# Attention probabilities: a diagonal of reciprocals in the transposing matmul, in place of a scaling pass

## The chip, the core and the metric

The kernel runs on one core of a Trainium2 chip. What counts is the device time of one execution in microseconds, as the median of three runs. The core has TensorE (PE, with its weight loads shown as PEld), VectorE (DVE), ScalarE (ACT), GpSimd (POOL) and SyncE (SP), which issues the transfers. Each engine works through its own queue in order.

## What is computed

Two layers of a diffusion backbone, over 1024 latent tokens and 256 context tokens. The first layer projects the input once and feeds two mixers side by side, a bidirectional chunked gated DeltaNet with 8 heads and windowed attention with 8 query heads on 2 key heads; the second layer is a gated linear recurrence. Both layers end in a squared-ReLU MLP. The part that matters here is the attention's softmax, which has one learned extra logit ("sink") per head:

```python
def _sink_softmax(scores, sink):
    s = jnp.broadcast_to(sink.astype(f32).reshape(1, KV_B, G_B, 1, 1), scores.shape[:-1] + (1,))
    p = jax.nn.softmax(jnp.concatenate([scores, s], axis=-1), axis=-1)
    return p[..., :-1]
...
        s_win = jnp.where(valid, jnp.einsum('bqkgd,bskd->bkgqs', q_blk, k_win) * scale, NEG_INF)
        s_ctx = jnp.einsum('bqkgd,bskd->bkgqs', q_blk, kc) * scale
        p = _sink_softmax(jnp.concatenate([s_win, s_ctx], axis=-1), sink)
        return (jnp.einsum('bkgqs,bskd->bqkgd', p[..., :span], v_win)
                + jnp.einsum('bkgqs,bskd->bqkgd', p[..., span:], vc))
```

A latent query block of 128 tokens sees up to three key blocks of its window and two blocks of cached context, so up to five key blocks of 128; a context query block sees two.

## The kernel before

**Stages.** The input projection and the triangular solves of the DeltaNet come first (to about 500 us), then one stage in which the DeltaNet's recurrence, the attention and the adaLN matmuls for later parts run interleaved (`dn_attention`, about 500 to 930 us), then the output projection, the MLPs and the second layer, which are long chains of three-term matmuls (L466 to L468, L546 to L548).

**The attention.** `attention` walks over 10 query blocks `a` and two halves `p` of the heads: 20 rounds. In a round, `att_scores` makes four score tiles of 128 queries (two key heads, two query heads each): matmuls L1918, L1921 and L1923 into a PSUM tile, a maximum on VectorE (L1925), an exp on ScalarE with the row sum (L1928) into an SBUF tile of tag `aP`, of which there are seven. Then the tiny tile `es` (128x4) takes the sink's share and the sums, and its reciprocal is taken (L1938). Line L1945 multiplies each of the four probability tiles by its column of `es`, two on VectorE and two on POOL (`ENG["P"]` is `"vvpp"`).

`att_out` follows one round later (`ATT_LAG` is 1). For each key block it transposes the four probability tiles on TensorE, with the identity as the moving operand (L1955), into one PSUM bank of tag `ps_w`, of which there are three, copies that bank to SBUF (tile `wraw`, on VectorE or ScalarE in turn), and multiplies it by the values for the two key heads (L1959). Over all rounds there are 84 key blocks: 5 for six of the query blocks, 4 for two and 2 for two, each twice. So there are 336 transposes and 168 matmuls on L1959. The last copy writes the result `x` to the mixer's output.

**The DeltaNet beside it.** Names in the rows: L1715, L1723 and L1731 prepare a chunk (`PT`, `Y`, `XW`), and L1762, L1769 and L1772 are a step of the recurrence, with copies of `VS` and the update of the state `S` on VectorE and ScalarE, and the products `St`, `QI`, `ek` and `kt` on POOL (a helper, L1638). `oA` and `oB` are outputs of the recurrence. The copies on ScalarE and VectorE are the helper lines L1643 and L1645. L1808 transposes a finished output. L300 are the adaLN matmuls, with weights `adaw` of 512 KB each from memory.

**What sets the order.** The parts are written as generators that are stepped in turn, each with a priority, and a list scheduler then fixes one order for each engine's queue. So an edit of the attention can also move instructions of its neighbours.

## Time and profile before

| | |
|---|---|
| Median of 3 runs | 3235.19 us (3234.73 to 3238.5) |
| The profiled execution | 3233.86 us, of which the span of the profile is 3232.1 us |
| Mean granted TensorE clock in it | 0.972 |
| PE busy | 3060.8 us, 95% |
| DVE, ACT, POOL busy | 1864.1 us, 1209.4 us, 1117.5 us |

How to read it: the busy share is an average over stages with different limits, so the stage that a change touches has to be looked at by itself. "Busy" for PE counts from an instruction's start to its modelled end, and neighbours overlap. The chain of work that ended last is followed back from the last instruction, at each step to what released it. A wait for several semaphores is put down to the engine that came last by the profile, which can be wrong by a little; where this matters the single instructions have to be read.

### The profile page before, as it was taken

To read this page: it belongs to the slowest core of one execution; us is meant where nothing else is said; L and a number is where in the kernel's file an instruction comes from. 1 tells how busy PE (TensorE), PEld (TensorE's weight loads), DVE (VectorE), ACT (ScalarE), POOL (GpSimd) and SP (SyncE) were. 2 spreads that over 40 slices of the span, in tenths; PEclk is the share of its full clock that TensorE was granted. 3 is DMA by queue.
4 is the path that set the end of the run, shared out by engine and by line. 5 is a ranking of instruction groups with operands and counts; after the bars stand their busy time and mean duration, and the time that the engine had idled before them with its cause. 6 is when DMAs were issued, how large, how long until landed. Compare 5 with 4: busy or idle time off the path is not lost.

```text
span 3232.1 us, 50272 instructions
## 1 busy us (share of the span) xinstructions
PE 3060.8 (95%) x19927; PEld 2485.3 (77%) x19927; DVE 1864.1 (58%) x2952; ACT 1209.4 (37%) x1972; POOL 1117.5 (35%) x781
## 2 busy tenths in 40 slices
PE   8989975889989999999999998999899999999999
PEld 5776764565557788888888877888678888888888
DVE  5548887576751522223777766888352222277776
ACT  5555433454331411112333335878241111133332
POOL 0000004454531432334767641000133333287664
PEclk9999986999999999999999998999999999999999
DMA  5346677536871233334534230110313333454332
GB/s 205 85 142 175 172 180 188 156 124 208 245 239 52 69 127 127 127 127 170 181 110 157 84 106 24 37 45 25 108 46 139 120 123 119 153 191 149 128 107 85
DMA packets 274058, 416.53 MB, mean 129 GB/s; under 512 B 77210, under 2 KB 139450, under 8 KB 269726
## 3 DMA queue, kind: packets, MB, share of 16 engines
q1 hardware_dynamic: 273822, 413.31, 40.0%
q8 instruction: 157, 2.57, 0.3%
q14 instruction: 79, 0.65, 0.1%
HBM read 290.80 MB, written 122.41 MB: 128 GB/s over the span
## 4 chain that ended last, share of the span: by engine, by line
PE 74%; DVE 8%; DMA 3%; issue 3%; ACT 2%; POOL 2%; SPq 1%; DVEq 0%; POOLq 0%; ACTq 0%
PE ps_mm L467 14%; PE ps_mm L466 14%; PE ps_mm L468 13%; PE ps_w L546 4%; PE ps_w L547 4%; PE ps_w L548 4%; PE ps_mm L547 4%; PE ps_mm L548 4%; PE ps_mm L546 4%; DVE prod L1600 2%; PE ps_ad L300 2%; PE ps_w L1959 1%; DVE Vinv L1601 1%; PE ps_w L1955 1%; PE ps_s L1918 1%
## 5 line engine op out<-in xcount | busy, mean ns | idle before, releaser
L466 PE MATMUL ps_mm<-hhi,whi 128*128 128x512 f32 (+2 forms) x2768 | 991.0, 359 | 24.7 <-ACT hhi L686 13.5
L467 PE MATMUL ps_mm<-hlo,whi 128*128 128x512 f32 (+2 forms) x2768 | 990.2, 358 | 8.8 <-POOL hlo L427 8.8
L468 PE MATMUL ps_mm<-hhi,wlo 128*128 128x512 f32 (+2 forms) x2768 | 987.6, 357 | 1.6 <-POOL wlo L457 1.6
L466 PEld LDWEIGHTS ps_mm<-hhi,whi 128*128 128x128 f32 (+1 forms) x2768 | 525.8, 190 | 111.1 <-ACT hhi L686 13.9
L467 PEld LDWEIGHTS ps_mm<-hlo,whi 128*128 128x128 f32 (+1 forms) x2768 | 526.2, 190 | 90.7 <-POOL hlo L427 11.6
L468 PEld LDWEIGHTS ps_mm<-hhi,wlo 128*128 128x128 f32 (+1 forms) x2768 | 526.3, 190 | 81.8 <-issue 6.0
L507 DVE TENSOR_TENSOR hid<-ffr 128x512 f32<-128x512 f32 (+1 forms) x192 | 148.9, 777 | 589.3 <-ACT ffr L506 507.1
L536 POOL TENSOR_TENSOR wlo<-ar,whi 128x1024 fp32r<-128x1024 f32 x96 | 246.7, 2584 | 268.7 <-ACT whi L535 251.2
L506 ACT ACTIVATE ffr<-ps_mm 128x512 f32<-128x512 f32 (+1 forms) x192 | 100.6, 525 | 548.2 <-PE ps_mm L468 546.5
L526 DVE SCALAR_TENSOR_TENSOR x<-ps_mm,mod,x 128x512 f32<-128x512 f32 x272 | 200.4, 746 | 82.8 <-PE ps_mm L548 82.6
L526 DVE SCALAR_TENSOR_TENSOR x<-ps_w,mod,x 128x512 f32<-128x512 f32 (+1 forms) x304 | 185.6, 632 | 100.7 <-PE ps_w L548 100.5
L511 POOL TENSOR_TENSOR tt<-hid 128x512 f32<-128x512 f32 x64 | 83.3, 1301 | 414.0 <-DVE hid L507 414.0
L453 ACT CAST whi<-wraw 128x512 fp32r<-128x512 f32 (+1 forms) x237 | 136.7, 617 | 197.9 <-PE ps_mm L467 84.1
L535 ACT CAST whi<-ar 128x1024 fp32r<-128x1024 f32 x96 | 98.0, 1051 | 292.6 <-PE ps_w L547 208.3
L457 POOL TENSOR_TENSOR wlo<-wraw,whi 128x512 fp32r<-128x512 f32 (+1 forms) x93 | 139.1, 1515 | 186.1 <-DVE hlo L687 93.0
L828 POOL MEMSET pad<- 128x2 f32 (+2 forms) x60 | 3.9, 119 | 439.8 <-DVE xc L846 200.0
L457 DVE TENSOR_TENSOR wlo<-wraw,whi 128x512 fp32r<-128x512 f32 x144 | 136.2, 972 | 33.2 <-ACT whi L453 33.0
L546 PE MATMUL ps_w<-pp,whi 128*128 128x256 f32 x512 | 143.6, 283 | 4.6 <-DVE x L526 4.6
L547 PE MATMUL ps_w<-pp,whi 128*128 128x256 f32 x512 | 143.4, 283 | 0.0
L548 PE MATMUL ps_w<-pp,wlo 128*128 128x256 f32 x512 | 141.0, 283 | 0.0
L511 POOL TENSOR_TENSOR tt<-hid,tt 128x512 f32<-128x512 f32 x64 | 85.3, 1333 | 118.2 <-DVE hid L507 118.0
L702 DVE SCALAR_TENSOR_TENSOR x<-ps_mm,mod,x 128x512 f32<-128x512 f32 (+1 forms) x40 | 25.9, 655 | 150.3 <-PE ps_mm L468 138.5
(416 smaller groups left out, 5890.1 us busy)
## 6 DMA issues: line engine op xcount, KB each, us to landing
adaw<-ada SPq DMA_DIRECT2D x80, 512.0 KB
dh<-hid SPq DMA_DIRECT2D x64, 640.0 KB
wraw<-ff SPq DMA_DIRECT2D x128, 256.0 KB
dt<-tt SPq DMA_DIRECT2D x32, 1024.0 KB
br<-dh SPq DMA_DIRECT2D x128, 256.0 KB
ar<-ff SPq DMA_DIRECT2D x128, 256.0 KB
br<-dt SPq DMA_DIRECT2D x128, 256.0 KB
wraw<-w_in SPq DMA_DIRECT2D x76, 256.0 KB
```

The costliest lines, as they stand in the source:

```text
L453: nc.scalar.copy(hv[:, o:o + half], raw[:, :half])
L457: e.tensor_tensor(lv[:, o:o + half], raw[:, :half], hv[:, o:o + half], op=ALU.subtract)
L466: nc.tensor.matmul(ps, whi[:, k, :], hhi[:, k, :], start=first and k == k0, stop=False)
L467: nc.tensor.matmul(ps, whi[:, k, :], hlo[:, k, :], start=False, stop=False)
L468: nc.tensor.matmul(ps, wlo[:, k, :], hhi[:, k, :], start=False, stop=last and k == k1 - 1)
L507: nc.vector.tensor_tensor(hid[i][:, t0:t0 + tw], r[:, :tw], r[:, :tw], op=ALU.mult)
L511: nc.gpsimd.tensor_tensor(t[:, j], x, y, op=ALU.subtract)
L526: nc.vector.scalar_tensor_tensor(xt[ti][:, o, :], ps[:, :tw], Gt[:, o, cc:cc + 1], xt[ti][:, o, :], op0=ALU.mult, op1=ALU.add)
L536: nc.gpsimd.tensor_tensor(lo[:, c], s, hi[:, c], op=ALU.subtract)
L546: nc.tensor.matmul(ps, ah, bh, start=first, stop=False, skip_group_check=True)
L547: nc.tensor.matmul(ps, ah, bl, start=False, stop=False, skip_group_check=True)
L548: nc.tensor.matmul(ps, al, bh, start=False, stop=last, skip_group_check=True)
```

## The change

The scaling pass over the four probability tiles goes. Instead, one POOL multiply per round writes `dg`, four diagonal matrices of 128x128 side by side: the identity times each of the four columns of reciprocals. Its tile `adg` has one buffer. `att_out` then uses an ordinary matmul with `dg` as the moving operand where it had a transpose with the identity: the probabilities are the stationary operand as before, and the product is the transposed tile with its columns already divided.

```diff
@@ -1936,23 +1936,20 @@
     nc.vector.tensor_tensor(es, es, sub(den), op=ALU.add)
     nc.vector.reciprocal(es, es)
-    for i in range(4):
-        P, sc = Ps[i][:, :w], es[:, i // 2, i % 2:i % 2 + 1]
-        e = ENG["P"][i]
-        if e == "a":
-            nc.scalar.activation(P, P, AF.Copy, scale=sc)
-        else:
-            (nc.vector if e == "v" else nc.gpsimd).tensor_scalar(P, P, sc, None, op0=ALU.mult)
-    yield Ps, kts
-
-
-def att_out(g, a, p, Ps, kts, mix):
+    dg = tl("adg", [128, 4, 128], 1)
+    nc.gpsimd.tensor_tensor(dg, g.con["ident"].unsqueeze(1).to_broadcast([128, 4, 128]),
+                            bc(es.rearrange("p k g -> p (k g)"), 128), op=ALU.mult)
+    yield Ps, dg, kts
+
+
+def att_out(g, a, p, Ps, dg, kts, mix):
...
-            nc.tensor.transpose(pt[:, 128 * j:128 * j + 128], Ps[j][:, 128 * i:128 * i + 128], g.con["ident"])
+            nc.tensor.matmul(pt[:, 128 * j:128 * j + 128], Ps[j][:, 128 * i:128 * i + 128], dg[:, j, :], start=True, stop=True,
+                             skip_group_check=True)
```

Since lines go, later lines move: L1955 becomes L1951, L1959 becomes L1956, and the multiply that makes `dg` is L1940.

The scheduler makes a slightly different order of it. POOL's queue in the middle of the stage, two rounds, before:

```order
L1638 TENSOR_TENSOR ek<-kt,sch 128x512
L1945 TENSOR_SCALAR aP<-aP,aes 128x640 x2
L1638 TENSOR_TENSOR kt<-kt,sch 128x512
L1638 TENSOR_TENSOR QI<-ql,qe 64x4x2x64
L1638 TENSOR_TENSOR St<-S_4629,egl 128x256
L1638 TENSOR_TENSOR QI<-ql,qe 64x4x2x64
L1638 TENSOR_TENSOR ek<-kt,sch 128x512
L1638 TENSOR_TENSOR kt<-kt,sch 128x512
L1945 TENSOR_SCALAR aP<-aP,aes 128x640 x2
```

and after the change:

```order
L1638 TENSOR_TENSOR ek<-kt,sch 128x512
L1638 TENSOR_TENSOR kt<-kt,sch 128x512
L1940 TENSOR_TENSOR adg<-con,aes 128x512
L1638 TENSOR_TENSOR QI<-ql,qe 64x4x2x64 x2
L1638 TENSOR_TENSOR St<-S_4629,egl 128x256
L1638 TENSOR_TENSOR ek<-kt,sch 128x512
L1638 TENSOR_TENSOR kt<-kt,sch 128x512
L1940 TENSOR_TENSOR adg<-con,aes 128x512
```

The two scalings of a round become one multiply. In the first of the two rounds it stands one place later than the scalings stood, behind `kt`, and the two `QI` products are no longer parted by `St`.

TensorE's queue there, from the preparation of a chunk up to the next step of the recurrence, before:

```order
L1955 MATMUL ps_w<-con,aP 128x128 x4
L1731 MATMUL ps_w<-XW,ek 64x64 x16
L1723 MATMUL ps_w<-XW,Y 32x32 x9
L1959 MATMUL ps_w<-wraw,Vtok 64x256 x2
L1723 MATMUL ps_w<-XW,Y 32x32 x7
L1955 MATMUL ps_w<-con,aP 128x128 x4
L1731 MATMUL ps_w<-XW,ek 64x64 x16
L1959 MATMUL ps_w<-wraw,Vtok 64x256 x2
L1955 MATMUL ps_w<-con,aP 128x128 x8
L1959 MATMUL ps_w<-wraw,Vtok 64x256 x2
L1955 MATMUL ps_w<-con,aP 128x128 x4
L1959 MATMUL ps_w<-wraw,Vtok 64x256 x2
```

and after the change:

```order
L1731 MATMUL ps_w<-XW,ek 64x64 x16
L1723 MATMUL ps_w<-XW,Y 32x32 x16
L1951 MATMUL ps_w<-adg,aP 128x128 x4
L1731 MATMUL ps_w<-XW,ek 64x64 x16
L1956 MATMUL ps_w<-wraw,Vtok 64x256 x2
L1951 MATMUL ps_w<-adg,aP 128x128 x8
L1956 MATMUL ps_w<-wraw,Vtok 64x256 x2
L1951 MATMUL ps_w<-adg,aP 128x128 x4
L1956 MATMUL ps_w<-wraw,Vtok 64x256 x2
L1951 MATMUL ps_w<-adg,aP 128x128 x4
L1956 MATMUL ps_w<-wraw,Vtok 64x256 x2
```

The first block of transposes has moved behind the whole of L1723, and the blocks and the value matmuls L1959 (now L1956) still take turns. In the other half of the period, where the recurrence steps, the order is the same as before.

## Rows read from the trace of the kernel before

**Rows 1.** The page's part 1: busy time, share of the span, instructions of each engine.

```profile
PE 3060.8 (95%) x19927; PEld 2485.3 (77%) x19927; DVE 1864.1 (58%) x2952; ACT 1209.4 (37%) x1972; POOL 1117.5 (35%) x781
```

**Rows 2.** The page's part 4: the chain that ended last, by engine.

```profile
PE 74%; DVE 8%; DMA 3%; issue 3%; ACT 2%; POOL 2%; SPq 1%; DVEq 0%; POOLq 0%; ACTq 0%
```

**Rows 3.** Busy time by window: length, engines (instructions), granted clock, DMA share, GB/s.

```profile
500.00:580.00 80.00, 55.99 (x641) 36.18 (x641) 60.31 (x113) 28.98 (x62) 37.48 (x29) 0.76 0.75 203
580.00:780.00 200.00, 175.03 (x2572) 123.20 (x2572) 134.32 (x267) 95.99 (x223) 102.24 (x82) 0.97 0.45 142
780.00:930.00 150.00, 145.45 (x1881) 84.65 (x1877) 106.28 (x263) 55.67 (x142) 68.83 (x57) 0.98 0.85 254
```

**Rows 4.** The same windows for line L1945 alone: the sum over them.

```profile
sum 430.00, DVE 27.57 POOL 70.25; mean DVE 9.19 POOL 23.42
```

**Rows 5.** Line L1945: its POOL instructions, and who waited for it (us, times).

```profile
L1945 POOL TENSOR_SCALAR aP<-aP,aes x40: 919/1880/2933, 545.1 to 922.0; 128x640 f32<-128x640 f32 x24, 128x512 f32<-128x512 f32 x8, 128x256 f32<-128x256 f32 x8
...
  PE ps_w L1769: 1.3, 4
```

**Rows 6.** PE's waits from 580 to 780 us: us in total, times, longest.

```profile
PE ps_ad L300 <- DMA adaw<-ada: 7.1, 2, 5.0
PE ps_w L1955 <- ACT oA L1643: 5.0, 4, 1.3
PE ps_w L1959 <- DVE wraw L1645: 4.0, 4, 1.7
PE ps_w L1955 <- ACT XW L1643: 3.8, 4, 1.3
...
PE ps_w L1769 <- POOL aP L1945: 1.3, 4, 0.3
```

**Rows 7.** Timeline around 668 us, VectorE and PE: start, us, engine, line, instruction.

```profile
667.82 0.43 DVE L1645 COPY VS<-ps_w 64x256 f32<-64x256 f32 x1
...
668.34 0.35 PE L1769 MATMUL ps_w<-VS,kt 64*64 64x64 f32 x5 [0.32 <-POOL aP L1945]
```

**Rows 8.** The chain from 500 to 930 us, pieces on L1945: start, us, what.

```profile
664.05 4.04 POOL aP L1945 x2
...
804.12 1.02 DVE aP L1945 x2
...
889.56 2.22 DVE aP L1945 x2
```

**Rows 9.** POOL's groups from 500 to 930 us: busy us, mean ns, idle before.

```profile
L1638 POOL TENSOR_TENSOR kt<-kt,sch 128x512 f32<-128x512 f32 x20 | 21.4, 1074 | 0.5
...
L1945 POOL TENSOR_SCALAR aP<-aP,aes 128x512 f32<-128x512 f32 x8 | 14.4, 1812 | 12.1 <-DVE aes L1938 8.8 <-DVE mod L310 3.2
```

**Rows 10.** Timeline of one block of L1955 and L1959, first part and whole.

```profile
671.90 0.33 PE L1955 MATMUL ps_w<-con,aP 128*128 128x128 f32 x1
...
671.90 0.66 PE L1955 MATMUL ps_w<-con,aP 128*128 128x128 f32 x4
...
673.29 0.44 PE L1959 MATMUL ps_w<-wraw,Vtok 128*64 128x256 f32 x2
...
673.29 0.65 PE L1959 MATMUL ps_w<-wraw,Vtok 128*64 128x256 f32 x4
```

**Rows 11.** Lines L1955 and L1959, matmuls: count, ns min/median/max, first and last start.

```profile
L1955 PE MATMUL ps_w<-con,aP x336: 270/273/476, 549.4 to 927.3; 128*128 128x128 f32 x168
...
L1959 PE MATMUL ps_w<-wraw,Vtok x336: 379/382/689, 554.5 to 930.3; 128*64 128x256 f32 x168
```

**Rows 12.** Windows for line L1955 alone: length, PE and PEld busy (instructions), clock.

```profile
500.00:580.00 80.00, 5.60 (x32) 3.52 (x32) 0.76 0.75 203
580.00:780.00 200.00, 32.37 (x196) 21.36 (x196) 0.97 0.45 142
780.00:930.00 150.00, 18.02 (x108) 11.64 (x108) 0.98 0.85 254
```

**Rows 13.** Tile VS: VectorE's copies from the state, ns min/median/max.

```profile
L1645 DVE COPY VS<-S x39: 273/600/2774, 505.1 to 915.9; 64x256 f32<-64x256 f32 x39
```

More of the change, by code (lines that the diff above doesn't have):

```diff
@@ L1987 @@
 ENG = dict(ek="p", kt="p", qe0="p", qe1="p", Y0="v", Y1="v", X0="a", X1="a", W0="a", W1="a", S0="a", S1="v", st="p", V0="a", V1="v",
-           o="a", pT="avava", ao="a", sq="v", os="v", P="vvpp")
+           o="a", pT="avava", ao="a", sq="v", os="v")
 def kernel(**inputs):
```

## Prediction, made before the changed kernel was run

> **What bounds the kernel now.** I read the page's busy line first: TensorE is busy 95% of the span [rows 1], and the chain that ended last lies on PE for 74% and on POOL for 2% [rows 2]. Of this chain only one stage can change, the DeltaNet and attention stage between 500 and 930 us, since every instruction that the diff touches stands there. I cut the stage in three by its engines [rows 3]. From 500 to 580 us PE is busy 56.0 of 80 us at a mean clock of 0.76. From 580 to 780 us it is busy 175.0 of 200: 25.0 us idle. From 780 to 930 us it is busy 145.5 of 150: 4.5 us idle, because the adaLN matmuls fill it. No other engine comes near: VectorE has 134.3 of 200 and 106.3 of 150, POOL 102.2 and 68.8. So the question at each edit is whether it touches PE, or something that PE waits for.
>
> **The scaling that goes.** L1945 takes 70.25 us on POOL and 27.57 on VectorE [rows 4], two instructions on each for every one of 20 rounds. Did PE wait for them? The list of those who waited for L1945 has one line of PE's matmuls, the DeltaNet line L1769 with 1.3 us [rows 5]; the transposes L1955, which read the scaled probabilities, are not in it. PE's own waits between 580 and 780 us say the same: the transposes wait for ScalarE's copies (oA 5.0 us, XW 3.8 us) and no row has them wait for aP [rows 6]. The 1.3 us put down to POOL's aP have another cause, too: POOL's pair of scalings starts at 664.05 and takes 4.04 us [rows 8], so it ends at 668.09, while PE's start at 668.34 follows VectorE's copy of VS, which ends at 668.25 [rows 7]. So the four pieces of 4.04 us that the chain shows for POOL (one stands in [rows 8]) aren't waits that end with the scaling. By its direct path the removal gives 0. What it can give is room on VectorE: the copy of VS stands behind a scaling pair and two maxima in VectorE's queue, and the 1.3 us of PE are really waits for it. I take 2 us for the stage (bounds 0 and 19.4 us, the latter the chain's four POOL pieces and its two VectorE pieces of 1.02 and 2.22 us [rows 8]).
>
> **The diagonal that comes.** Twenty POOL multiplies of 128x512, one operand broadcast along its rows, the other repeated four times. No row has this form. The nearest is kt, 128x512 with one broadcast operand, 1.07 us; the farthest is the scaling of 128x512 itself, 1.81 us [rows 9]. I take 1.07: 20 x 1.07 = 21 us in place of 70.25, ready after one instruction instead of after two in a row (4.04 us). POOL has idle time in all three stretches, so its price on the path is 0. There is one buffer for it: the multiply waits until the transposes of the round before have read the last diagonal, and QI and St of the recurrence stand behind it in POOL's queue. But it also needs the reciprocals, and these need the fourth exp of its own round. A round takes four aP buffers and there are seven, so this exp waits for the round before to release its first one, and that happens in the last block of the same set of transposes. The extra wait is then a few matmuls; bounds 0 and 20 x 0.66 = 13 us if a whole block each time [rows 10]. I take 0.
>
> **The matmul in place of the transpose.** This is on PE and decides the case. A transpose of 128 columns costs 0.11 us once PE streams: one is in flight 0.33 us, four 0.66, so three more take 0.33 [rows 10]. Is a plain fp32 matmul of the same shape dearer? The counts say so: L1955 issues 84 key blocks x 4 = 336 transposes and leaves 336 records; L1959 issues 84 x 2 = 168 matmuls and also leaves 336 [rows 11]. A plain fp32 matmul is thus two passes, a transpose one. The length of a pass: the two first passes of L1959, which run side by side in the two halves of the array, take 0.44 us, and with both second passes 0.65, so a pass of 256 columns adds 0.21, or 0.105 for 128 columns [rows 10]: the transpose's own rate. So the new matmul is 0.22 us where the transpose was 0.11: 0.44 us more per key block. Bounds: below, 0 (if the second pass were hidden; nothing in L1959's rows hides it); above, 0.66, a whole block as it stands alone. I take 0.44, and 84 x 0.44 = 37 us in all.
>
> The Trainium skill speaks here too: "TensorE: Matmul & The Clock Gate", section Terms, says that the transpose mode is four times faster for FP32. By it a block would rise from 0.44 to 1.76 us instead of 0.88, and the term would be an estimated 84 x 1.32 = 111 us. The rows above give a factor of two; the rule has its place among the rivals.
>
> **What hides it.** Divided over the three stretches by the transposes seen there [rows 12]: 32 of them are 8 blocks, 3.5 us; 196 are 49 blocks, 21.6 us; 108 are 27 blocks, 11.9 us. The order of work on PE is nearly what it was, so the waits that I know keep their places, and a wait shrinks only by what is added between the event that starts it and the instruction that waits.
> - 580 to 780 us: the four waits for oA (5.0 us) and the bank behind it have two transposing blocks ahead of them, 0.88 us each: 3.5 us. The four waits for VectorE's wraw (4.0 us) have one or two: about 2.6. The waits of L1769 (1.3 us) have one: all of it. The 3.8 us for XW stand in front of the transposes, and the 7.1 us for adaLN loads have few of them: 0 [rows 6]. Hidden 7.4, and 2 from VectorE's room: 21.6 - 7.4 - 2 = 12.
> - 780 to 930 us: 4.5 us are idle at all. I take half as cover, 2.4: 9.5 remain.
> - 500 to 580 us: PE is idle 24 us; the clock is low, so a block can cost twice its 0.44 us. I take 2 of 3.5 as hidden: 1.5.
>
> Sum 12 + 9.5 + 1.5 = 23 us. The profiled execution took 3233.86 us, 1.76 more than its span and 1.3 less than the median of the three runs. Forecast 3233.9 + 23 = 3257. Its own range: if the first two stretches hide everything and the third its 4.5 us, 11.9 - 4.5 = 7.4, that is 3241; if nothing is hidden, 3271.
>
> **Rivals.**
> 1. Faster: VectorE and POOL set the pace and PE's 95% is padding. For it: VectorE's copies VS<-S are 0.27 us at best, 0.60 at the median and 2.77 at worst [rows 13], so other work stretches them, and POOL's load falls by 49 us. Then the 19.4 us of scaling on the chain go, four diagonals of 1.07 come back, 15 us are won, and PE's 37 us lie in waits up to 2 us in the last stretch: 3233.9 - 15 + 2 = 3221. It wins once more than 22 of the 37 us are hidden and the whole 15 are real. Against it: the transposes wait for aP nowhere, and 11.9 us meet only 4.5 idle ones.
> 2. No difference: the hidden part and VectorE's room just balance the 37 us, or the two-pass matmul costs no more than a transpose here: 3234. Against it: the counts of records.
> 3. Nothing hidden, 3271, the end of my forecast's own range and counted in it.
> 4. A matmul dearer than two passes: at four times the transpose's 0.11 us each of 84 blocks grows by 1.32 us, 111 us in all, less some 15 of cover: 3330. Against it: the records and the pass time of L1959. This is the result that the Trainium skill's rule above would give.
>
> **How the numbers follow.** Forecast (3241 to 3271) 0.78; rival 1 0.09; rival 2 0.11; rival 4 0.02. About 0.2% (6.5 us around 3235) is what a measurement of this kernel can tell from no change. So slower 0.79 (the forecast with rival 4, less its lowest edge), same 0.12, faster 0.09. The range runs from the upper edge of rival 2, 3236, to 3271: the forecast and a little of rival 2, about 0.8.
>
> **What would show it.** After the change L1951 should leave 672 matmul records, not 336, with four matmuls taking some 1.1 us; no L1945 on POOL or VectorE, and 20 multiplies near 1.07 us on POOL. PE's busy time should rise by about 35 us and the stage end 23 us later; from 780 us on PE should have next to no idle time. POOL's and VectorE's busy time should fall by some 49 and 28 us with nothing gained by it. I am wrong if L1951 leaves 336 records, if its blocks are as short as before, or if the stretch from 580 to 780 us gets shorter, since then VectorE or POOL set its pace.

## The result

The changed kernel takes 3255.97 us (median of 4 runs, 3253.44 to 3258.53), against 3236.14 us for the kernel before beside it. The ratio is 1.0061, with a 95% interval of 1.0043 to 1.0078. So it is slower by about 20 us. The forecast was 3257 us, with the range 3236 to 3271.

The span and the first part of the changed kernel's page, to stand beside [rows 1]:

```profile
span 3253.3 us, 50889 instructions
PE 3091.4 (95%) x20263; PEld 2529.6 (78%) x20263; DVE 1843.6 (57%) x2912; ACT 1208.9 (37%) x1972; POOL 1071.1 (33%) x761
```

TensorE is busy 30.6 us longer, VectorE 20.5 us less and POOL 46.4 us less. The 336 extra instructions on PE (20263 against 19927) are the second passes. The windows of [rows 3] now:

```profile
500.00:580.00 80.00, 55.86 (x705) 40.03 (x707) 58.52 (x110) 25.98 (x57) 33.92 (x26) 0.77 0.73 197
580.00:780.00 200.00, 188.69 (x2729) 145.09 (x2724) 118.50 (x245) 97.43 (x225) 69.35 (x69) 1.00 0.45 137
780.00:930.00 150.00, 143.84 (x1802) 90.50 (x1800) 93.42 (x224) 53.13 (x134) 54.21 (x49) 0.99 0.81 235
```

From 580 to 780 us PE's idle time fell from 25.0 to 11.3 us. Before 580 and from 780 us on it did not fall. The line of the new matmul, its matmuls and its weight loads: count, ns min/median/max, first and last start; and the POOL multiply that makes the diagonals:

```profile
L1951 PEld LDWEIGHTS ps_w<-adg,aP x672: 186/192/338, 550.2 to 954.7; 128*128 128x128 f32 x168
L1951 PE MATMUL ps_w<-adg,aP x672: 271/275/534, 550.4 to 954.8; 128*128 128x128 f32 x168
...
L1940 POOL TENSOR_TENSOR adg<-con,aes x20: 1039/1041/1822, 547.1 to 944.8; 128x512 f32<-128x512 f32 x20
```

336 matmuls leave 672 records where the transposes left 336 [rows 11]. The multiply takes 1.04 us at the median, and nobody is listed as waiting for it. A block of four matmuls, eight records, and two blocks in a row, from the timeline of PE (start, us):

```profile
677.58 1.16 PE L1951 MATMUL ps_w<-adg,aP 128*128 128x128 f32 x8
...
681.40 2.05 PE L1951 MATMUL ps_w<-adg,aP 128*128 128x128 f32 x16
```

A block takes 1.16 us where it took 0.66 [rows 10]; in a row a further one adds 0.89, which is 0.111 us for each pass. Over the whole stage, 500 to 960 us, the line and its predecessor, from the groups of the costliest instructions (busy us, mean ns | idle before). Before:

```profile
L1955 PE MATMUL ps_w<-con,aP 128*128 128x128 f32 x336 | 56.0, 290 | 11.4 <-ACT oA L1643 5.0 <-ACT XW L1643 3.8 <-DVE oB L1781 2.1
```

and after:

```profile
L1951 PE MATMUL ps_w<-adg,aP 128*128 128x128 f32 x672 | 95.7, 289 | 2.4 <-DVE oB L1781 1.3 <-ACT oA L1643 1.2
```

39.7 us of matmul came in, and 9.0 us of idle time in front of these instructions went. PE's waits from 580 to 780 us in the changed kernel, to compare with [rows 6], show the same:

```profile
PE ps_w L1731 <- ACT XW L1643: 3.4, 4, 1.8
PE ps_w L1956 <- DVE wraw L1645: 3.2, 4, 0.9
PE ps_ad L300 <- DMA adaw<-ada: 3.1, 1, 3.1
PE ps_w L1956 <- ACT wraw L1643: 0.7, 2, 0.5
PE ps_w L1951 <- ACT oA L1643: 0.3, 1, 0.3
```

The waits for `oA` fell from 5.0 to 0.3 us, those for adaLN weights from 7.1 to 3.1, and the wait of L1769 is gone. The waits for VectorE's `wraw` fell little, from 4.0 to 3.2, and those for `XW` moved from the transposes (3.8) to L1731 (3.4).

**Where the 20 us arise.** To compare the two traces at the same work, I cut them at the start of the 8th, 24th and 40th of the 40 steps of the recurrence (L1762). Windows of the kernel before between these steps, columns as in [rows 3]:

```profile
606.82:753.59 146.77, 129.94 (x2019) 96.86 (x2017) 104.03 (x206) 79.93 (x185) 79.02 (x64) 0.98 0.39 120
753.59:922.41 168.82, 162.18 (x2142) 94.83 (x2139) 118.48 (x289) 62.07 (x156) 80.51 (x66) 0.98 0.83 251
```

and of the changed kernel:

```profile
608.03:761.77 153.74, 145.95 (x2179) 116.82 (x2176) 95.17 (x192) 78.84 (x183) 55.14 (x56) 1.00 0.38 115
761.77:946.19 184.42, 177.73 (x2273) 110.55 (x2271) 110.89 (x267) 63.50 (x159) 63.44 (x57) 0.99 0.80 241
```

Up to the 8th step the changed kernel has lost 1.2 us. In the middle part PE does 16.0 us more, but its idle time falls from 16.8 to 7.8 us, so the part grows by 7.0 us only. In the last part PE does 15.6 us more, its idle time stays at 6.7 us, and the part grows by the whole 15.6. At the end of the stage 3 us come back, so the first matmul of the output projection starts 20.7 us later. After it nothing differs: the spans differ by 21.2 us.

**A third term, the clock.** The last columns but two of these windows are the granted clock, 1.0 for the upper level of 2.4 GHz and 0.5 for the lower of 1.2. It is a mean, so a stretch of length L at a mean clock c spent 2(1-c)L at the lower level. The two kernels from 580 us to the first matmul of the output projection, before:

```profile
580.00:943.50 363.50, 329.77 (x4492) 210.33 (x4492) 248.59 (x541) 156.62 (x372) 173.94 (x141) 0.97 0.63 192
```

and after:

```profile
580.00:964.20 384.20, 361.56 (x4832) 250.97 (x4827) 228.68 (x511) 158.47 (x376) 131.34 (x124) 0.99 0.61 184
```

The lower level fell from 22 to 8 us. One place shows how. In both kernels TensorE waits for a load of adaLN weights shortly after 580 us, then runs four matmuls of L300. Before (timeline; start, us, what, and the idle time ahead of it):

```profile
583.40 1.92 PE L300 MATMUL ps_ad<-adaw,sc 128*32 128x512 f32 x4 [4.96 <-DMA adaw<-ada]
```

and after:

```profile
586.06 1.05 PE L300 MATMUL ps_ad<-adaw,sc 128*32 128x512 f32 x4 [3.14 <-DMA adaw<-ada]
```

The same four matmuls took 1.92 us behind the longer wait and 1.05 behind the shorter one. The windows of these places show the granted clock (third number from the end): during the longer wait it fell, and the matmuls behind it ran at 0.50. Before, the wait and the matmuls:

```profile
578.40:583.40 5.00, 0.04 (x1) 0.00 (x0) 2.59 (x5) 1.71 (x4) 3.58 (x2) 0.86 0.81 242
583.40:585.30 1.90, 1.90 (x6) 0.23 (x6) 0.00 (x0) 0.00 (x0) 0.45 (x1) 0.50 0.97 379
```

and after, the matmuls:

```profile
586.06:587.00 0.94, 0.94 (x4) 0.14 (x4) 0.00 (x0) 0.00 (x0) 0.00 (x0) 1.00 0.79 322
```

The Trainium skill ("TensorE: Matmul & The Clock Gate", section "HAM oscillation — how this bites in real kernels") says that idle gaps of TensorE bring its clock down; these rows agree.

### The profile page after: what moved, and what is told of

The parts are those of the page before. It is cut to its first block, busy times and chain, and to the rows that moved or that the text cites. A ratio compares the mean times of both kernels' runs of the same rounds, so it can differ in the third digit from the quotient of the medians.

```text
span 3253.3 us, 50889 instructions
## 1 busy us (share of the span) xinstructions
PE 3091.4 (95%) x20263; PEld 2529.6 (78%) x20263; DVE 1843.6 (57%) x2912; ACT 1208.9 (37%) x1972; POOL 1071.1 (33%) x761
## 4 chain that ended last, share of the span: by engine, by line
PE 76%; DVE 8%; DMA 4%; issue 3%; ACT 2%; SPq 1%; POOL 1%; DVEq 0%; ACTq 0%; POOLq 0%
PE ps_mm L466 13%; PE ps_mm L467 13%; PE ps_mm L468 13%; PE ps_w L546 4%; PE ps_w L547 4%; PE ps_w L548 4%; PE ps_mm L547 4%; PE ps_mm L548 4%; PE ps_mm L546 3%; PE ps_w L1951 2%; DVE prod L1600 2%; PE ps_ad L300 2%; PE ps_w L1956 1%; DMA adaw<-ada 1%; DVE Vinv L1601 1%
## 5 line engine op out<-in xcount | busy, mean ns | idle before, releaser
L457 DVE TENSOR_TENSOR wlo<-wraw,whi 128x512 fp32r<-128x512 f32 x144 | 136.2, 973 | 33.9 <-ACT whi L453 33.7
L541 DVE TENSOR_TENSOR bl<-br,bh 128x1024 fp32r<-128x1024 f32 x56 | 101.6, 1814 | 12.0 <-ACT bh L540 10.7
```

The source lines that it names most:

```text
L457: e.tensor_tensor(lv[:, o:o + half], raw[:, :half], hv[:, o:o + half], op=ALU.subtract)
```

## The experiments

My theory after the result: TensorE's passes set the price, the exchange of the scaling for the diagonal is worth nothing, and idle time hides part of the passes. The first rival: the scaling's removal wins some 15 us, and the passes cost nearly all of their 40.

**All runs in one table.** Each ratio is to runs of the kernel before that were taken beside that kernel. It isn't the quotient of the medians, and can differ from it by a few us. The columns from "length" on are of one profiled execution each, which can lie up to 8 us from the median. They cover 580 us to the first matmul of the output projection and come from window rows like the two above. "Low" is the time at the lower clock level, good to 4 us, since the mean clock has two digits. "Work" is PE's busy time less half of "low": about what it would be at the upper level.

| Kernel | Median, us | Ratio to before (95%) | Length | PE busy | PE idle | Clock | Low | Work |
|---|---|---|---|---|---|---|---|---|
| before | 3236.14 | 1 | 363.5 | 329.8 | 33.7 | 0.97 | 22 | 319 |
| changed | 3255.97 | 1.0061 (1.0043 to 1.0078) | 384.2 | 361.6 | 22.6 | 0.99 | 8 | 358 |
| changed, again | 3252.21 | 1.0056 (1.0041 to 1.0072) | 385.9 | 362.3 | 23.6 | 1.00 | 0 | 362 |
| matmul alone | 3256.57 | 1.0065 (1.0051 to 1.0079) | 393.3 | 366.4 | 26.9 | 0.98 | 16 | 359 |
| half of the matmuls | 3242.32 | 1.0011 (0.9998 to 1.0024) | 372.9 | 349.1 | 23.8 | 0.97 | 22 | 338 |
| identity per round | 3237.37 | 1.0009 (0.9997 to 1.0021) | 371.1 | 337.0 | 34.1 | 0.94 | 45 | 315 |
| no division | 3223.14 | 0.9971 (0.9957 to 0.9985) | 353.4 | 326.0 | 27.4 | 0.97 | 21 | 315 |
| diagonal unread | 3231.73 | 0.9987 (0.9976 to 0.9997) | 360.0 | 327.8 | 32.2 | 0.97 | 22 | 317 |
| all scaling on VectorE | 3248.77 | 1.0048 (1.0029 to 1.0067) | 375.5 | 334.9 | 40.6 | 0.95 | 38 | 316 |
| division at the end | 3239.79 | 1.0011 (1.0002 to 1.0019) | 370.1 | 336.8 | 33.3 | 0.96 | 30 | 322 |
| transposed twice | 3251.32 | 1.0053 (1.0035 to 1.0071) | 382.7 | 354.0 | 28.7 | 0.99 | 8 | 350 |
| transposed thrice | 3283.55 | 1.0145 (1.0127 to 1.0162) | 414.4 | 390.9 | 23.5 | 0.98 | 17 | 383 |
| F32R, one pass | 3268.85 | 1.0099 (1.0083 to 1.0115) | 396.7 | 353.8 | 42.9 | 0.91 | 71 | 318 |
| F32R, twice | 3267.89 | 1.0108 (1.0088 to 1.0129) | 395.0 | 367.1 | 27.9 | 0.97 | 24 | 355 |

The work column sorts the kernels by passes: 315 to 322 us where the probabilities pass once, 338 with half of the second passes, 350 to 362 where they pass twice, 383 with three. What the time makes of it is decided by the idle and the low column.

### The matmul alone, scaling kept

```diff
-            nc.tensor.transpose(pt[:, 128 * j:128 * j + 128], Ps[j][:, 128 * i:128 * i + 128], g.con["ident"])
+            nc.tensor.matmul(pt[:, 128 * j:128 * j + 128], Ps[j][:, 128 * i:128 * i + 128], g.con["ident"], start=True, stop=True,
+                             skip_group_check=True)
```

> The kernel before, its scaling kept, with one edit: the transposes of the probabilities become plain fp32 matmuls by the identity. Theory (the second pass on TensorE sets the price, the scaling costs nothing): the whole rise of the changed kernel is here already, 3256 to 3261 us, with 672 matmul records and four matmuls of a block near 1.16 us. Rival (the scaling's removal is worth 15 us, and the second pass costs all of its 35 to 40 us): 3268 to 3275 us, since nothing pays for it here. If the rise were due to the diagonal or to the order of work, this would stay near 3236.

Measured: 3256.57 us, ratio 1.0065. The whole rise is here, with no diagonal in the program and the scaling still in it. The rival's 3268 to 3275 is excluded.

### No division at all

```diff
-    for i in range(4):
-        P, sc = Ps[i][:, :w], es[:, i // 2, i % 2:i % 2 + 1]
...
-            (nc.vector if e == "v" else nc.gpsimd).tensor_scalar(P, P, sc, None, op0=ALU.mult)
```

> The kernel before without the four scalings of the probabilities, transposes by the identity kept; this leaves the division by the sum out of the computation. Theory (nobody on the path waits for the scaling, some 2 us of room on VectorE at most): 3231 to 3236 us, VectorE's and POOL's busy time down by 28 and 70 us with TensorE's unchanged. Rival (VectorE and POOL set the pace of the stage): the 15 to 19 us of scaling on the chain go, 3217 to 3222 us.

Measured: 3223.14 us, ratio 0.9971 (0.9957 to 0.9985). That is 9 us faster by the ratio and 13 by the medians: more than the theory's 0 to 5, and only 1 us above the band of the rival, so this time by itself does not refute the rival. The identity per round, below, does. The gain is made between 500 and 580 us. The first transposes start at 533.7 us there (line L1948 of this kernel), while before they start at 549.4 [rows 11]:

```profile
L1948 PE MATMUL ps_w<-con,aP x336: 270/273/476, 533.7 to 922.7; 128*128 128x128 f32 x168
```

Once nothing divides, a transpose waits only for its own tile's exp, and the scheduler puts the first ones into time in which TensorE idles beside a busy VectorE. The fifth step of the recurrence then starts at 571.9 us against 586.2 before, and nothing further is won after it: of these 14 us, 10 are left where the output projection starts (933.4 and 943.5). So this kernel tests two edits at once, the scaling and the dependence of the transposes on the reciprocals. The change keeps that dependence, through the diagonal.

### The diagonal made and read by nobody

```diff
-            nc.tensor.matmul(pt[:, 128 * j:128 * j + 128], Ps[j][:, 128 * i:128 * i + 128], dg[:, j, :], start=True, stop=True,
-                             skip_group_check=True)
+            nc.tensor.transpose(pt[:, 128 * j:128 * j + 128], Ps[j][:, 128 * i:128 * i + 128], g.con["ident"])
```

(against the changed kernel)

> The changed kernel with its diagonal made on POOL and read by nobody, the probabilities transposed by the identity; this leaves the division by the sum out of the computation. It differs from the kernel before by the scaling that goes and the POOL multiply that comes. Theory (both are off the path): as without any division, 3231 to 3236 us. If the diagonal multiply delays the recurrence's work in POOL's queue: up to 13 us more than without any division, 3244 to 3249 us. Rival (VectorE and POOL set the pace): 3217 to 3225 us.

Measured: 3231.73 us, ratio 0.9987, within the theory's bounds. It has the same flaw: the transposes no longer wait for the reciprocals, and the fifth step starts at 572.9 us. Set against the kernel without division it prices the POOL multiply at about 5 us (0.9987 less 0.9971; 9 by the medians), with intervals that overlap.

### The second pass alone taken away

To keep the dependence, this kernel makes in each round an identity of its own, in the diagonal's tile, at the diagonal's cost, and transposes by it:

```diff
-    nc.vector.reciprocal(es, es)
+    nc.vector.tensor_scalar(es, es, 0.0, None, op0=ALU.mult)
...
-                            bc(es.rearrange("p k g -> p (k g)"), 128), op=ALU.mult)
+                            bc(es.rearrange("p k g -> p (k g)"), 128), op=ALU.add)
...
-            nc.tensor.matmul(pt[:, 128 * j:128 * j + 128], Ps[j][:, 128 * i:128 * i + 128], dg[:, j, :], start=True, stop=True,
-                             skip_group_check=True)
+            nc.tensor.transpose(pt[:, 128 * j:128 * j + 128], Ps[j][:, 128 * i:128 * i + 128], dg[:, j, :])
```

(against the changed kernel)

> The changed kernel with the second pass alone taken away: the reciprocal becomes a product with zero and the POOL multiply an addition to the identity, so that each round makes an identity of its own in the diagonal's tile at the diagonal's cost and time, and the transposes by it wait for it as the matmuls do; this leaves the division by the sum out of the computation. Theory (the price is the second pass, the exchange of scaling for diagonal is worth about nothing as long as the transposes still wait for the reciprocals): 3233 to 3238 us, and the changed kernel's 20 us more are all second passes. Rival (the scaling's removal is worth 9 us by itself, as the kernel without division suggests): 3225 to 3229 us, and the second passes cost some 29 us. If the wait for the one diagonal buffer costs: above 3240 us.

Measured: 3237.37 us, ratio 1.0009 (0.9997 to 1.0021): 3 us more than before, with zero in the interval. The rival's 3225 to 3229 is excluded. So with the dependence kept, the exchange of the scaling for the diagonal wins nothing, and the second pass is worth 1.0061 less 1.0009, some 17 us, out of 40 us of matmul. The moved order of TensorE is in this price too: as in the changed kernel, the first block of transposes stands behind the preparation of the chunk here, and idle time (34.1 us against 33.7 before) is not hidden by it.

This kernel and the one before it both leave out the scaling and make a tile of the diagonal's size at its cost. They differ in whether the transposes wait for it. So that dependence is worth 1.0009 less 0.9987, some 7 us (6 by the medians), with intervals that only touch: much of what the kernel without division won.

### The same work from plain transposes: twice and thrice

```diff
-            nc.tensor.transpose(pt[:, 128 * j:128 * j + 128], Ps[j][:, 128 * i:128 * i + 128], g.con["ident"])
+            for _ in range(2):
+                nc.tensor.transpose(pt[:, 128 * j:128 * j + 128], Ps[j][:, 128 * i:128 * i + 128], g.con["ident"])
```

(and with `range(3)`; scaling kept, run beside the changed kernel once more)

> The kernel before with every transpose of the probabilities issued twice into the same place, scaling kept: 672 single passes, TensorE's work as in the changed kernel, nothing else new. Theory (the price is TensorE's passes, whatever their form): 37 us more of TensorE's work, about half of it covered as in the changed kernel, 3252 to 3261 us. If the plain fp32 form, its weight load or the diagonal costs by itself: 3236 to 3246 us here.

> As the one with every transpose twice, but three times: 1008 passes, twice the added work, some 74 us. Theory (waits of TensorE and clock hide a fixed amount, 11 us of idle time and some 6 us of low clock, and the first 37 us have used it up): the second 37 us cost nearly in full, 30 to 37 us above the kernel with every transpose twice, 3284 to 3295 us. Rival (a fixed share of about half is hidden, since waits for other engines give way again): 3270 to 3278 us.

> The changed kernel once more beside the kernels with repeated transposes, for a closer interval and its granted clock. Theory: 3253 to 3259 us, a clock of 0.973 or more where the kernel before has 0.968 to 0.973, and no more than 3 us from the kernel with every transpose twice. Rival (scaling in exchange for diagonal is worth the 9 us that the kernel without division gained): 9 us below that kernel.

Measured: 3251.32, 3283.55 and 3252.21 us, each up to 1 us under its band, with the differences as the theory had them. Twice costs 17 us (ratio 1.0053), the change beside it 18 us (1.0056), and thrice 47 us (1.0145). The first addition of passes costs 17 us, the second, of the same size, 32 us by the medians and 30 by the ratios. The windows of these two kernels from 580 us on (twice first, then thrice) show why:

```profile
580.00:962.70 382.70, 354.02 (x4856) 242.78 (x4855) 249.15 (x546) 158.91 (x376) 175.01 (x143) 0.99 0.60 184
```

```profile
580.00:994.40 414.40, 390.94 (x5121) 275.77 (x5119) 237.30 (x545) 157.99 (x376) 177.27 (x144) 0.98 0.55 168
```

From the kernel before to twice, PE's idle time goes from 33.7 to 28.7 us and the low clock from 22 to 8. From twice to thrice only 5 us more of idle time go, the low clock wins nothing (8 to 17 us), and the length grows by 31.7 of 36.9 us more busy time. So over these two additions what hides passes is a nearly fixed amount, and not a share of half. That twice and the change agree within 1 us also says that the plain fp32 form, the diagonal and the scaling all together are worth next to nothing beside the count of passes. Singly they are not separated: the changed kernel has 8 us more work in the table than twice, and 6 us less idle time.

### Half of the matmuls

Tiles 0 and 1 through a diagonal of two blocks, tiles 2 and 3 scaled on VectorE and transposed:

```diff
-    for i in range(4):
+    dg = tl("adg", [128, 2, 128], 1)
+    nc.gpsimd.tensor_tensor(dg, g.con["ident"].unsqueeze(1).to_broadcast([128, 2, 128]), bc(es[:, 0, :], 128), op=ALU.mult)
+    for i in range(2, 4):
...
+            if j < 2:
+                nc.tensor.matmul(pt[:, 128 * j:128 * j + 128], Ps[j][:, 128 * i:128 * i + 128], dg[:, j, :], start=True, stop=True,
+                                 skip_group_check=True)
+            else:
+                nc.tensor.transpose(pt[:, 128 * j:128 * j + 128], Ps[j][:, 128 * i:128 * i + 128], g.con["ident"])
```

> Half of the change: tiles 0 and 1 of the probabilities are divided in a plain matmul by a diagonal, tiles 2 and 3 are scaled on VectorE and transposed. 336 second passes are halved to 168. Theory (a price for each second pass): about half of the rise, 3243 to 3250 us. If waits hide the first ones, as they would if idle time of TensorE covers a fixed amount, then less than half: 3236 to 3243 us. Rival (VectorE's or POOL's load decides): POOL has lost its scaling and VectorE keeps its own, so 3225 to 3236 us.

Measured: 3242.32 us, ratio 1.0011 (0.9998 to 1.0024): 4 us by the ratio and 6 by the medians, less than half of the rise either way, just under the theory's lower end and in the case it named for it, that waits hide the first passes. With the runs above: half of the added passes cost 4 to 6 us, all of them 17 to 20, double 47.

### All scaling on VectorE

```diff
-           o="a", pT="avava", ao="a", sq="v", os="v", P="vvpp")
+           o="a", pT="avava", ao="a", sq="v", os="v", P="vvvv")
```

> The kernel before with all four scalings of a round on VectorE and none on POOL: POOL loses its 70 us, VectorE's 28 us double. Theory (nobody on the path waits for the scaling): within 4 us of before, 3232 to 3240 us. If POOL's share of the scaling holds the stage up, the four scalings end sooner (4 x 0.69 us in place of 4.04 us) and it is faster, 3224 to 3231 us. If VectorE sets the pace, 28 us more on it cost 10 to 28 us: 3246 to 3264 us.

Measured: 3248.77 us, ratio 1.0048, 13 us slower by the medians and 15 by the ratio. The theory's "within 4 us" fell; it came out as in the case in which VectorE sets the pace. Its 80 scalings take 0.55 us at the median (first fence), and two of PE's waits from 580 to 780 us, not seen in [rows 6] at that size, are now for the exp that stands behind VectorE's maxima, and for VectorE's copy of `VS` (second fence):

```profile
L1945 DVE TENSOR_SCALAR aP<-aP,aes x80: 345/547/555, 547.1 to 933.1; 128x640 f32<-128x640 f32 x48, 128x512 f32<-128x512 f32 x16, 128x256 f32<-128x256 f32 x16
```

```profile
PE ps_s L1918 <- ACT aP L1928: 3.9, 4, 1.3
PE ps_w L1769 <- DVE VS L1645: 2.0, 5, 0.5
```

PE's work is what it was (316 us), but its idle time rose by 7 us and the low clock by 16. So VectorE is not free: more load on it costs. Where it costs is read from the waits and not tested by itself, since the order of TensorE's work moved too. Less load on VectorE, as in the change, won nothing that could be measured.

### F32R, one pass and two

F32R is a 4-byte type like fp32, in which this kernel holds the mask of the scores. Probabilities and diagonal in F32R make the plain matmul a single pass (`tl("aP", [128, 640], ..., F32R)`, and the same for `adg`):

```diff
-        P = tl("aP", [128, 640], g.NB["aP"])
+        P = tl("aP", [128, 640], g.NB["aP"], F32R)
...
-    dg = tl("adg", [128, 4, 128], 1)
+    dg = tl("adg", [128, 4, 128], 1, F32R)
```

(against the changed kernel; the second kernel issues each matmul of this one twice)

> The changed kernel with the probabilities and the diagonal written as F32R, so that the product is rounded further. Theory (the price is passes of TensorE): if such a matmul leaves one record, 336 in all, and a block takes no longer than with transposes (0.66 us alone), then 3228 to 3238 us, as without the second pass; if F32R at 128 columns takes longer than a transpose, then as the changed kernel or above, 3256 us and more. Rival (diagonal, order or buffers cost the time): 3250 to 3258 us however long a block is.

> The kernel with probabilities and diagonal in F32R, each of its single-pass matmuls issued twice into the same place: 672 passes in place of 336, 37 us more work for TensorE. Theory (the single F32R pass was slow for its idle gaps, after which the granted clock fell to the lower level for 71 us of the stage; a second pass fills them): no slower than with one pass although the work rises, 3250 to 3262 us, with the clock of the stretch from 580 us on back at 0.98 or more. Rival (the F32R form or its weight load is dear by itself): the 37 us come on top, at least in part, 3285 to 3305 us. Between, 3265 to 3280 us, would mean that the clock gives back only part.

Measured: 3268.85 us with one pass, ratio 1.0099, and 3267.89 with two, ratio 1.0108. The single pass did leave 336 records, and a block took 0.66 us, as a transpose does, and yet the kernel is 13 us slower than the changed one. None of its three cases had said this. Where it goes, at one place in the timeline of the first kernel: a block at full clock, then a wait of 3.98 us, then two blocks that take 2.24 us, and one that takes 1.12.

```profile
599.79 0.66 PE L1951 MATMUL ps_w<-adg,aP 128*128 128x128 f32 x4
...
607.97 2.24 PE L1951 MATMUL ps_w<-adg,aP 128*128 128x128 f32 x8 [3.98 <-ACT oA L1643]
...
611.20 1.12 PE L1951 MATMUL ps_w<-adg,aP 128*128 128x128 f32 x4
```

The windows there, with PE's busy time as the second number and the clock third from the end:

```profile
600.00:605.00 5.00, 3.99 (x86) 3.42 (x85) 1.80 (x6) 1.16 (x3) 0.00 (x0) 1.00 0.70 210
605.00:610.00 5.00, 2.01 (x8) 1.83 (x8) 2.84 (x7) 1.55 (x4) 2.30 (x3) 0.69 0.49 151
610.00:615.00 5.00, 5.00 (x22) 2.94 (x23) 2.44 (x3) 1.77 (x4) 3.52 (x4) 0.50 0.19 52
```

TensorE was busy 2.01 of 5 us, and then ran the next 5 us wholly at 1.2 GHz. Over the stage it had 42.9 us of idle time and 71 us at the lower level. With every matmul twice, PE's busy time at full clock is 37 us more (355 against 318), and the time is the same within the runs: idle time fell to 27.9 us and the low clock to 24. That is neither the theory's 3250 to 3262 nor the rival's 3285 to 3305, but a time in the case between, in which the clock gives back only part. Idle time and clock together made up for all of the added work, and yet 12 us above the changed kernel remain.

**The order differs, too.** The kernel with one identity per round has the same count of passes as F32R with one pass, but less idle time (34.1 against 42.9 us), less low clock (45 against 71) and 31 us less time. TensorE's order is not the same in the two. At the place above, F32R runs two steps of the recurrence (L1769, L1772) with no block of probabilities between them. The second of them is in the fence, and the block behind it is the one that waits 3.98 us for `oA`:

```profile
602.70 0.68 PE L1769 MATMUL ps_w<-VS,kt 64*64 64x64 f32 x16
603.31 0.69 PE L1772 MATMUL ps_w<-VS,QI 128*64 128x64 f32 x16
```

With one identity per round this block stands ahead of the second of these steps:

```profile
599.78 0.66 PE L1951 MATMUL ps_w<-adg,aP 128*128 128x128 f32 x4
600.37 0.68 PE L1769 MATMUL ps_w<-VS,kt 64*64 64x64 f32 x16
600.98 0.69 PE L1772 MATMUL ps_w<-VS,QI 128*64 128x64 f32 x16
```

F32R with one pass has this exchange at four places (near 600, 684, 726 and 763 us); the identity per round and F32R with two passes have it at none of them. From 580 to 950 us TensorE's waits for `oA` in front of the blocks come to 8.9 us with one F32R pass and to 3.3 with the identity per round, and the list of F32R with two passes has none.

**What stays open:** between one F32R pass and two, the order changes along with the passes, so how much of the 37 us the added work itself gave back is not shown. Nor is it shown how much of the loss of the F32R form comes from this order and how much from the form.

### Division at the end

The experiments pointed to a version that frees the transposes from the division and makes it after the product with the values: reciprocals spread over the head's rows by four small matmuls per round, then one VectorE multiply in place of ScalarE's copy.

```diff
+        if i == len(kts) - 2:
+            for kv in range(2):
+                for k in range(2):
+                    nc.tensor.matmul(pr[64 * kv:64 * kv + 64, 128 * k:128 * k + 128], es[:, kv, k:k + 1].to_broadcast([128, 64]),
+                                     g.con["ident"], start=True, stop=True, skip_group_check=True)
+            rb = tl("arb", [128, 256], 1)
+            nc.scalar.copy(rb, pr)
...
-    copy(g, ENG["ao"], mix[ti][:, 4 + 2 * p:6 + 2 * p, c:c + 128], po.rearrange("p (g t) -> p g t", t=128))
+    nc.vector.tensor_tensor(mix[ti][:, 4 + 2 * p:6 + 2 * p, c:c + 128], po.rearrange("p (g t) -> p g t", t=128),
+                            rb.rearrange("p (g t) -> p g t", t=128), op=ALU.mult)
```

> Another place for the division, computing the whole reference: no scaling and no diagonal, transposes by the identity; four small matmuls per round (128 rows, 64 columns of a broadcast reciprocal as weights, the identity as moving operand) spread the reciprocals over the head's rows, ScalarE copies them out, and VectorE multiplies the finished output by them in place of ScalarE's copy. Theory (passes of TensorE count, and the transposes gain from no longer waiting for the division): the 9 us of the kernel without division, less 20 x 0.44 = 9 us of new matmuls partly covered, 3228 to 3236 us. Rival (only the order of work moved the kernel without division): 3236 to 3245 us.

Measured: 3239.79 us, ratio 1.0011 (1.0002 to 1.0019), in the band of the rival. By the same steps of the recurrence it leads the kernel before by 5.9 us at the 8th step, from the freed transposes, and loses that and more by the 40th, where it is 11.2 us behind; why is not settled. Unlike the expectation says, it changes part of the attention's output, so only its time is read here; it is no version to take over, and not a faster one either. No version tried beats the kernel before with the division in it.

## Why the prediction was right, point by point

**What bounds the stage.** Right: TensorE. Repeated transposes, which add nothing but passes, cost what the change costs (1.0053 and 1.0056).

**The scaling that goes, 0.** Right, by three differences in which the transposes wait for the reciprocals on both sides: the change against the matmul alone (1.0061 and 1.0065), the change against transposes twice (1.0056 and 1.0053), and the identity per round against before (1.0009). They give -1, +1 and +3 us for scaling out and diagonal in, each within some 4 to 8 us. The list of those who waited for L1945 [rows 5] had said it. This is the price of both together; the scaling alone, with the dependence kept, was not run. VectorE did get room: its copies of `VS` from the state [rows 13] went from 600 to 328 ns at the median, though the longest stayed at 2.8 us.

```profile
L1645 DVE COPY VS<-S x40: 273/328/2831, 484.2 to 938.7; 64x256 f32<-64x256 f32 x40
```

The 2 us that I had allowed for this room are too small to be seen in the runs. What I had overlooked is that the order of the program depends on what the transposes wait for: without that dependence 6 to 7 us were there to be won, in the stretch from 500 to 580 us. It didn't matter here, since the diagonal keeps the dependence.

**The diagonal, 1.07 us, 0 on the path.** The size is right: 1.04 us at the median, as `kt`, and nobody is listed as waiting for it. The 0 is not shown by itself: the two kernels without the dependence put some 5 us on the multiply, with intervals that overlap. The one buffer isn't tested by itself; the identity per round, which has the same buffer and the same wait, bounds diagonal and wait together by the 7 us at the top of its interval, plus what the scaling's removal may have given back.

**The second pass, 37 us.** Right in kind and somewhat too small: 39.7 us by the group, a block 0.50 us longer instead of 0.44. Plain transposes twice add up to 350 us of work in the table and the changed kernel to 358, so the plain form is a little dearer than two transposes. Its passes follow each other at 0.111 us, and its weight loads take 192 ns at the median, against 140 for the transposes:

```profile
L1956 PEld LDWEIGHTS ps_w<-con,aP x672: 137/140/231, 545.9 to 950.0; 128*128 128x128 f32 x168
L1956 PE MATMUL ps_w<-con,aP x672: 270/273/477, 545.9 to 950.1; 128*128 128x128 f32 x168
```

(these are of the kernel with every transpose twice). The factor is two and not the four of the Trainium skill's rule ("TensorE: Matmul & The Clock Gate", section Terms), so rival 4 is out.

**What hides it.** In the middle part I had 7.4 us of waits and 2 of VectorE's room, 9.4 together, and PE's idle time fell by 9.0 between the 8th and the 24th step. That they agree is partly luck. The waits for `oA` went from 5.0 to 0.3, more than the 3.5 that I had, and that of L1769 went as I had said. But VectorE's `wraw`, from which I had 2.6, gave 0.8, and the adaLN weights, from which I had 0, gave 4.0 from 580 to 780 us, though outside of these two steps. In the last part I had 2.4 of the 4.5 idle us as cover, and there was none: idle stayed at 6.7 us between the recurrence steps, and from 780 to 930 us it even rose, from 4.5 to 6.2. The sign that "from 780 us on PE should have next to no idle time" was wrong. The waits that are left from 780 to 950 us are mostly for others:

```profile
PE ps_ad L300 <- DMA adaw<-ada: 3.1, 4, 1.1
PE ps_w L1956 <- DVE wraw L1645: 2.1, 3, 1.2
```

By the forecast's own rule, a longer block makes the wait for adaLN weights shorter only where it stands between the load's start and L300; which blocks do was not looked up.

**The sum, 23 us.** It came out at 20.7 in the traces, and that it is so close is luck, since errors of a few us met. In the table the length is work, idle time and half of the low time. Work rose by 39 us, and 11.1 of idle time went (33.7 to 22.6). I had 37 of matmul and 13.8 hidden: 2 too little of the one and 2.7 too much of the other. Against these stands a term that my sum didn't have, the clock. From 580 us on the lower level fell by 14 us (22 to 8), of which at most half, 7 us, is won: 39 - 11.1 - 7 = 20.9. I had read 0.97 and 0.98 in [rows 3] and made nothing of them, though at the two places shown above the clock fell in such idle time as the matmuls were to fill. The split over the stretches was off as well: up to the 24th step the change costs 8.2 us, where I had 13.5 up to 780 us, and from there on 12.5, where I had 9.5.

**The rivals.** Rival 1 (faster, 3221): the kernel without division came to 3223, but in large part by the freed order, and it isn't what the change does. Rival 2 (no difference): excluded by the interval. Rival 3 (nothing hidden, 3271): excluded, some 20 of 40 us were hidden.

**The signs.** The records, the block and the multiply came out as said. PE's busy time rose by 30.6 us where I had about 35, POOL's fell by 46.4 where I had 49, and VectorE's by 20.5 where I had 28.

## What to carry to other kernels

Price work that is added to the engine which sets the pace in three terms: its own time, less the idle time in front of the instructions that grow, less what a clock that stays up gives back. Here the last two were a nearly fixed stock, and the next addition of the same size cost almost its whole time (17 us, then 32). A factor folded into a transposing fp32 matmul wasn't free although the work that it saved seemed large (70 us on POOL, 28 on VectorE): the transpose is one pass and the plain matmul two, and the saved work lay on engines that TensorE hardly waited for. An experiment that leaves a step out also cuts what waits for it: replace the step by a neutral one of the same cost that keeps the dependence (here an identity made anew in each round), or the order of the program answers in its place. And before two kernels are set against each other, compare the order of the pacing engine's work in their traces: with F32R it had moved.

## What the hardware showed that I had not expected

- **More work, same time.** Issuing each F32R matmul twice, 37 us more of TensorE's work, left the time as it was (3268.85 and 3267.89 us): TensorE's idle time fell from 42.9 to 27.9 us and its time at 1.2 GHz from 71 to 24. The order of its work changed as well, so the added work is not shown to be the only cause.
- **F32R weights load as slowly as fp32 ones in a plain matmul:** 192 ns at the median in both, against 140 ns in front of a transpose of the same 128 columns. The weight-load rows of the F32R kernel:

```profile
L1951 PEld LDWEIGHTS ps_w<-adg,aP x336: 186/192/338, 551.4 to 960.6; 128*128 128x128 f32 x168
L1951 PE MATMUL ps_w<-adg,aP x336: 272/276/476, 551.6 to 960.7; 128*128 128x128 f32 x168
```

- **A POOL multiply with two repeated operands** (identity and reciprocals, 128x512) takes 1.04 us at the median and 1.08 in the mean, about as long as `kt` with one, 1.07 in the mean [rows 9].
